# A decoder block on one core: sums copied out of PSUM first, block transfers on the GpSimd queue, the feed-forward in emission order

## The chip, the cores and the metric

The kernel runs on one core of a Trainium2 chip. The metric is device time in microseconds; before the change it was 1412.69 us, the median of three runs (1409.19 to 1413.38).

## What is computed

One layer of a decoder for 256 tokens of width 2048 in float32: an RMS norm, one wide projection, three attention branches whose results are gated, merged and projected back, and a feed-forward with a squared ReLU. The change lies in the feed-forward, the last line here:

```python
h = _rms(x, g_mix_norm[layer])
z = h @ w_in[layer]
...                                   # three attentions from z: oa, ob, oc
merged = (gates[:, :, 0] * (oa @ w_up_a[layer])
          + gates[:, :, 1] * (ob @ w_up_b[layer])
          + gates[:, :, 2] * (oc @ w_up_c[layer]))
x = x + merged @ w_out[layer]
h2 = _rms(x, g_ffn_norm[layer])       # 256 x 2048; w_ff_in is 2048 x 8192, w_ff_out 8192 x 2048
x = x + jnp.square(jax.nn.relu(h2 @ w_ff_in[layer])) @ w_ff_out[layer]
```

## The kernel before

**Matmuls and splits.** Every weight is split into two parts, `whi` (ScalarE casts it to float32r) and `wlo` (VectorE subtracts that from the weight), and so is every activation. A product is three passes: high by high, low by high, high by low. `wload` loads a plain weight tile (two 128-row slices of 512 columns) through SP's DMA queue into `raw` and splits it. The pools `raw`, `whi` and `wlo` have four buffers each. `wahead` keeps the splits of up to two further tiles written ahead of the matmuls of the current one, by the order of `plan`.

**Feed-forward.** The 8192 hidden columns are worked off in four quarters, q = 0 to 3. q = 0 has four plain strips of w_ff_in (`strip_rows`), two plain strips of w_ff_out and one unit of w_ff_out. Each later q has two units of w_ff_in and two of w_ff_out, so there are 13 units.

**A unit** (`unit`) computes 256 rows by 1024 columns. For six of its sixteen 128-row slices it uses a Winograd form of the 2 x 2 block product: seven block products instead of eight (B11, T2, T3, T1, B21, B22, T4), each in two parts of two slices and one slice (`SUBS`). The other ten slices come as ten plain tiles. `UNIT` is the order: B11, three plain, T2, plain, T3, plain, T1, plain, B21, plain, B22, plain, T4, two plain; with the parts counted singly 24 places, numbered 0 to 23. `uload` makes the block sums T3, T2, T1 and T4 of the weights on VectorE (1536 elements each) and splits them; the blocks lie in six `sraw` buffers that `fetch` fills, through SP's queue too. B11, T2, T3 and T1 go to PSUM banks of their own (`pp`): the first two in the pool `ps_sc`, T3 and T1 in `ps_tp`, which has two buffers and also serves the transposes. After T1 `early` combines these (`partial_sums`: `p1s`, `uu` twice, `wz`); in w_ff_out three additions into the residual `x1` follow. At the last two plain places `late` ends the four accumulators: in w_ff_in VectorE adds (`y`), and ScalarE takes ReLU and square; in w_ff_out VectorE adds into `x1`.

**Hidden tiles.** `hidden_rows` is a generator that `pump` moves on by one step after each place: transposes of a `y` on TensorE into a `tp` of `ps_tp`, then the split into `hid`. The tiles 0 and 1 of each q also give the activation sums of the next w_ff_out unit: `sums_of` reads both `tp` of such a tile straight from PSUM, with a copy `a21s` on ScalarE and four operations on VectorE, and splits the result into `ss`. `split_rows` does the same once for the input of w_ff_in (`sx`).

**What sets the order.** Nothing is ordered by hand: the scheduler of the framework puts each engine's instructions in an order that it works out with a timing model, and it may move an instruction ahead of others that were written earlier. The line numbers below are those of the profile; the helper `split_into` gives its lines 275 and 276 to whatever is split through it.

Of the kernel before, what the change touches and what calls it, by code (L numbers as in the profile page):

```python
# [11 lines left out]
F32 = mybir.dt.float32  # L12
F32R = mybir.dt.float32r
AF = mybir.ActivationFunctionType
ALU = mybir.AluOpType
# [3 lines left out]
P = 128  # L19
# [26 lines left out]
SH = 3  # L46
K1, K2 = [0, 1, 4], [2, 3, 5]
SUBS = [(0, 2), (2, 1)]
# [46 lines left out]
def tile_block(ctx: ExitStack, tc: tile.TileContext, io):  # L95
    nc = tc.nc
# [29 lines left out]
    posts, attn = deque(), deque()  # L126

    def step(queue):
        try:
            next(queue[0][1])  # L130
        except StopIteration:
            queue.popleft()
# [6 lines left out]
    def drain(queue, label):  # L139
        while any(l == label for l, _ in queue):  # L140
            step(queue)
# [26 lines left out]
    last_load = [None]  # L168
# [24 lines left out]
    def fetch(u, n):  # L193

        if u == len(units):
            return
        name, at = units[u]
        size = P * SH * 512
        got = ready.setdefault(u, {})
        for i, k in enumerate(list(BLOCKS)[len(got):n], len(got)):  # L200
            off = (at * len(BLOCKS) + i) * size
            got[k] = pool[0].tile([P, SH, 512], F32, tag="sraw", name="sraw")
            last_load[0] = nc.sync.dma_start(
                got[k], io[name][off:off + size].rearrange("(p g n) -> p g n", p=P, g=SH)).ins

    def uload(name, which):

# [64 lines left out]
    def split_into(hi, lo, src, scale=None):  # L272

        if scale is None:
            nc.scalar.copy(hi, src)  # L275
            nc.vector.tensor_tensor(lo, src, hi.bitcast(F32), op=ALU.subtract)  # L276
        else:
            nc.scalar.activation(hi, src, AF.Copy, scale=scale)  # L278
            nc.vector.scalar_tensor_tensor(lo, src, scale, hi.bitcast(F32), op0=ALU.mult, op1=ALU.subtract)

    def unit(name, sums, xh, xl, early, late):


# [359 lines left out]
    for t in range(2):  # L643
        nc.vector.scalar_tensor_tensor(zf[:, t, :], acc[t][:, 256:260], rstd[:, t:t + 1], bf,
                                       op0=ALU.mult, op1=ALU.add)
# [71 lines left out]
    ff = ctx.enter_context(tc.tile_pool(name="ff", bufs=1))  # L717
# [4 lines left out]
    for c in range(4):  # L722
# [6 lines left out]
        for j in range(2):  # L729
            tp = ps_tp.tile([P, 2, S], F32, tag="tp", name="tp")  # L730
# [18 lines left out]

    x1h, x1l = rows_of(x1T)  # L750

    S_USE = {"T1": 0, "T2": 1, "T3": 2, "B22": 3}

    def sums_of(a, ss):

        (a11, a12), (a21, a22) = a
        n = ss.shape[3]
        sf = ff.tile([P, 4, n, P], F32, tag="sf", name="sf", bufs=1)
        a21s = ff.tile([P, n, P], F32, tag="a21", name="a21s", bufs=1)
        nc.scalar.copy(a21s, a21)  # L760
        nc.vector.tensor_tensor(sf[:, 0], a22, a21s, op=ALU.add)  # L761
        nc.vector.tensor_tensor(sf[:, 2], a11, a21s, op=ALU.subtract)
        nc.vector.scalar_tensor_tensor(sf[:, 1], a11, -1.0, sf[:, 0], op0=ALU.mult, op1=ALU.add)
        nc.vector.tensor_tensor(sf[:, 3], a12, sf[:, 1], op=ALU.subtract)
        split_into(ss[:, 0], ss[:, 1], sf)

    def sums_for(at, ss):

        sums = {k: (lambda hl, g, i=i: ss[:, hl, i, g, :]) for k, i in S_USE.items()}
        sums["B11"] = lambda hl, g: at(K1[g], hl, slice(0, P))  # L770
# [4 lines left out]
    def partial_sums(p1, p6, p7, p5):  # L775
        p1s = ff.tile([P, 512], F32, tag="p1", name="p1s", bufs=1)
        uu = ff.tile([P, 2, 512], F32, tag="uu", name="uu", bufs=1)
        wz = ff.tile([P, 2, 512], F32, tag="wz", name="wz", bufs=1)
        nc.scalar.copy(p1s, p1)
        nc.vector.tensor_tensor(uu[:, 0, :], p6, p1s, op=ALU.add)  # L780
        nc.vector.tensor_tensor(uu[:, 1, :], p7, uu[:, 0, :], op=ALU.add)
        nc.vector.tensor_tensor(wz, p5[:, None, :].to_broadcast([P, 2, 512]), uu, op=ALU.add)
        return p1s, uu[:, 1, :], wz

    def hidden_rows(ys, hh, ss, wait):

        for _ in range(wait):
            yield
        tps = []
        for t in range(2):  # L790
            yield
            tp = ps_tp.tile([P, 4, P], F32, tag="tp", name="tp")
            for i in range(4):
                nc.tensor.transpose(tp[:, i, :], ys[t][:, i * P:(i + 1) * P], ident)  # L794
            ts = slice(t * P, (t + 1) * P)
            split_into(hh[:, :, 0, ts], hh[:, :, 1, ts], tp)
            tps.append(tp)
        if ss is not None:
            yield
            g0, n = SUBS[ss[1]]  # L800
            sums_of([[tp[:, n * i:n * i + n, :] for i in range(2)] for tp in tps], ss[0][:, :, :, g0:g0 + n, :])


    rrow = ff.tile([P, S], F32, name="rrow")
    sx = ff.tile([P, 2, 4, SH, P], F32R, name="sx")
# [16 lines left out]
            scaled.append(f)  # L822

    def split_rows():
        yield
        for g, f in enumerate(scaled):
            yield
            split_into(x1T[:, 4 * g:4 * g + 4, 0, :], x1T[:, 4 * g:4 * g + 4, 1, :], f)
            if g < len(SUBS):
                yield  # L830
                g0, n = SUBS[g]
                sums_of([[f[:, n * j:n * j + n, i * P:(i + 1) * P] for j in range(2)] for i in range(2)],
                        sx[:, :, :, g0:g0 + n, :])

    for q in range(4):
        hid = [ff.tile([P, 4, 2, S], F32R, tag="hid", name="hid", bufs=4) for _ in range(4)]
        ss = ff.tile([P, 2, 4, SH, P], F32R, tag="ss", name="ss", bufs=1)
        for sidx in range(4 if q == 0 else 0):
            if sidx == 1:
                attn.append(("x", scale_rows()))  # L840
            acc = strip_rows("w_ff_in", 512, KT, x1h, x1l)
            ys = []
            for t in range(2):
                y = ff.tile([P, 512], F32, tag="y", name="y", bufs=4)
                nc.scalar.activation(y, acc[t], AF.Relu, scale=ss2[:, t:t + 1])
                nc.scalar.activation(y, y, AF.Square)
                ys.append(y)
            posts.append(("h", hidden_rows(ys, hid[sidx], (ss, sidx) if sidx < len(SUBS) else None, 1)))
        for u in range(2 if q else 0):
            more = {}  # L850

            def early(*p):
                more[0, 0], more[0, 1], wz = partial_sums(*p)
                more[1, 0], more[1, 1] = wz[:, 0, :], wz[:, 1, :]

            def late(c, t, acc):
                y = ff.tile([P, 512], F32, tag="y", name="y", bufs=4)
                nc.vector.tensor_tensor(y, acc, more[c, t], op=ALU.add)
                nc.scalar.activation(y, y, AF.Relu)
                nc.scalar.activation(y, y, AF.Square)  # L860
                more["y", t] = y
                if t:
                    i = 2 * u + c
                    posts.append(("h", hidden_rows([more["y", 0], y], hid[i], (ss, i) if i < len(SUBS) else None,
                                                   0 if c else 2)))

            unit("w_ff_in", sums_for(lambda kt, hl, ts: x1T[:, kt, hl, ts], sx), x1h, x1l, early, late)
        if q == 0:
            drain(attn, "x")
            attn.append(("x", split_rows()))  # L870
        hidh = lambda kt, t: hid[kt // 4][:, kt % 4, 0, t * P:(t + 1) * P]
        hidl = lambda kt, t: hid[kt // 4][:, kt % 4, 1, t * P:(t + 1) * P]
        for c in range(0 if q else 2):
            acc = strip_rows("w_ff_out", 512, KT, hidh, hidl)
            cs = slice(c * 512, (c + 1) * 512)
            for t in range(2):
                nc.vector.tensor_tensor(x1[:, t, cs], acc[t], x1[:, t, cs], op=ALU.add)
        for u in range(0 if q else 1, 2):
            cols = [slice(1024 * u + 512 * c, 1024 * u + 512 * (c + 1)) for c in range(2)]

            def early(*p):
                p1s, u3, wz = partial_sums(*p)
                nc.vector.tensor_tensor(x1[:, 0, cols[0]], p1s, x1[:, 0, cols[0]], op=ALU.add)
                nc.vector.tensor_tensor(x1[:, 1, cols[0]], u3, x1[:, 1, cols[0]], op=ALU.add)
                nc.vector.tensor_tensor(x1[:, :, cols[1]], wz, x1[:, :, cols[1]], op=ALU.add)

            def late(c, t, acc):
                nc.vector.tensor_tensor(x1[:, t, cols[c]], acc, x1[:, t, cols[c]], op=ALU.add)  # L888
                if q == 3:
                    load(io["out"][t * P:(t + 1) * P, cols[c]], x1[:, t, cols[c]])  # L890

            unit("w_ff_out", sums_for(lambda kt, hl, ts: hid[kt // 4][:, kt % 4, hl, ts], ss), hidh, hidl, early, late)
        drain(attn, "x")
# [71 lines left out]
```

## Time and profile before

| | us |
|---|---|
| median of three runs | 1412.69 |
| profiled execution | 1411.21 |
| span of that execution | 1409.4 |
| TensorE busy | 1393.0 (99%) |
| VectorE busy | 1024.9 (73%) |
| ScalarE busy | 759.9 (54%) |
| GpSimd busy | 37.5 (3%) |

The first unit starts at about 842 us. From there on VectorE is busy for nine tenths of the time, TensorE nearly throughout. In the profile PE is TensorE, DVE VectorE, ACT ScalarE and SP the engine whose queue carries nearly all loads. A matmul's end is modelled and overlaps the next one's start, so that the distance between starts is its cost, not its duration. "Idle before" names the engine whose work ended the wait.

### The profile page before, as it was taken

To read this page: it belongs to the slowest core of one execution; us is meant where nothing else is said; L and a number is where in the kernel's file an instruction comes from. 1 tells how busy PE (TensorE), PEld (TensorE's weight loads), DVE (VectorE), ACT (ScalarE), POOL (GpSimd) and SP (SyncE) were. 2 spreads that over 40 slices of the span, in tenths; PEclk is the share of its full clock that TensorE was granted. 3 is DMA by queue.
4 is the path that set the end of the run, shared out by engine and by line. 5 is a ranking of instruction groups with operands and counts; after the bars stand their busy time and mean duration, and the time that the engine had idled before them with its cause. 6 is when DMAs were issued, how large, how long until landed. Compare 5 with 4: busy or idle time off the path is not lost.

```text
span 1409.4 us, 17262 instructions
## 1 busy us (share of the span) xinstructions
PE 1393.0 (99%) x6343; PEld 1153.1 (82%) x6343; DVE 1024.9 (73%) x1167; ACT 759.9 (54%) x983; POOL 37.5 (3%) x41
## 2 busy tenths in 40 slices
PE   8999999999999999999999999999999999999998
PEld 6888888888888888888888888878888788887887
DVE  6647657566755646565567758899988899988996
ACT  7545545466444444444455635566555665556653
POOL 0211102000000000000000000000000000000000
PEclk9999999999999999999999999999999999999999
DMA  9747555655566666676675755655666556665562
GB/s 326 239 139 239 169 148 165 197 184 165 182 207 198 199 200 200 196 233 204 183 231 180 228 188 185 219 186 176 200 210 198 172 184 206 207 191 181 187 207 77
DMA packets 75524, 274.54 MB, mean 195 GB/s; under 512 B 8624, under 2 KB 9392, under 8 KB 75184
## 3 DMA queue, kind: packets, MB, share of 16 engines
q1 hardware_dynamic: 75296, 273.42, 60.6%
q8 instruction: 50, 0.82, 0.2%
q14 instruction: 34, 0.28, 0.1%
q10 hardware_dynamic: 144, 0.02, 0.0%
HBM read 271.31 MB, written 2.10 MB: 194 GB/s over the span
## 4 chain that ended last, share of the span: by engine, by line
PE 73%; DVE 0%; ACT 0%; issue 0%
PE acc L265 33%; PE acc L292 31%; PE pp L292 8%; PE tp L794 1%; PE tp L734 0%; PE tp L706 0%; DVE hid L276 0%; ACT hid L275 0%; DVE sf L761 0%; ACT a21s L760 0%; DVE x L888 0%; PE rr L813 0%
## 5 line engine op out<-in xcount | busy, mean ns | idle before, releaser
L188 DVE TENSOR_TENSOR wlo<-raw,whi 128x1024 fp32r<-128x1024 f32 (+2 forms) x425 | 509.6, 1204 | 283.1 <-ACT whi L187 274.2
L187 ACT CAST whi<-raw 128x1024 fp32r<-128x1024 f32 (+2 forms) x425 | 441.3, 1039 | 455.9 <-PE acc L265 313.7
L265 PE MATMUL acc<-whi,xT 128*128 128x512 f32 (+1 forms) x1472 | 393.6, 389 | 5.7 <-ACT xT L278 5.4
L265 PEld LDWEIGHTS acc<-whi,xT 128*128 128x128 f32 x1472 | 272.7, 189 | 61.5 <-ACT xT L278 6.1
L265 PE MATMUL acc<-wlo,xT 128*128 128x512 f32 (+1 forms) x736 | 226.2, 388 | 0.0
L275 ACT CAST whi<-sraw 128x1024 fp32r<-128x1024 f32 (+1 forms) x182 | 151.0, 837 | 115.3 <-PE acc L292 83.4
L276 DVE TENSOR_TENSOR wlo<-sraw,whi 128x1024 fp32r<-128x1024 f32 (+1 forms) x182 | 169.8, 953 | 22.2 <-ACT whi L275 16.4
L292 PE MATMUL acc<-whi,hid 128*128 128x512 f32 x644 | 166.4, 391 | 0.0
L265 PEld LDWEIGHTS acc<-wlo,xT 128*128 128x128 f32 x736 | 136.9, 188 | 28.1 <-issue 1.0
L292 PE MATMUL acc<-whi,x1T 128*128 128x512 f32 x552 | 140.7, 391 | 0.0
L292 PEld LDWEIGHTS acc<-whi,hid 128*128 128x128 f32 x644 | 120.3, 188 | 24.5
L292 PEld LDWEIGHTS acc<-whi,x1T 128*128 128x128 f32 x552 | 103.2, 188 | 21.2
L292 PE MATMUL acc<-wlo,hid 128*128 128x512 f32 x322 | 91.1, 390 | 0.0
L292 PE MATMUL acc<-wlo,x1T 128*128 128x512 f32 x276 | 76.9, 390 | 0.0
L292 PEld LDWEIGHTS acc<-wlo,hid 128*128 128x128 f32 x322 | 60.2, 188 | 12.4
L265 PE MATMUL acc<-whi,x1T 128*128 128x512 f32 x256 | 70.0, 394 | 0.0
L265 PE MATMUL acc<-whi,mT 128*128 128x512 f32 x256 | 69.9, 392 | 0.0
L265 PE MATMUL acc<-whi,oT 128*128 128x512 f32 x224 | 60.0, 390 | 0.6 <-ACT oT L278 0.6
L292 PEld LDWEIGHTS acc<-wlo,x1T 128*128 128x128 f32 x276 | 51.6, 188 | 10.6
L265 PEld LDWEIGHTS acc<-whi,mT 128*128 128x128 f32 x256 | 47.9, 188 | 9.6
L265 PEld LDWEIGHTS acc<-whi,x1T 128*128 128x128 f32 x256 | 47.5, 188 | 9.4
L265 PEld LDWEIGHTS acc<-whi,oT 128*128 128x128 f32 x224 | 42.0, 188 | 9.6 <-ACT oT L278 0.9
(201 smaller groups left out, 1337.5 us busy)
## 6 DMA issues: line engine op xcount, KB each, us to landing
raw<-in_w_gate_dram SPq DMA_DIRECT2D x96, 512.0 KB, 3.6
raw<-in_w_ff_in_dram SPq DMA_DIRECT2D x92, 512.0 KB, 4.1
raw<-in_w_ff_out_dram SPq DMA_DIRECT2D x86, 512.0 KB, 4.3
raw<-in_w_proj_dram SPq DMA_DIRECT2D x77, 512.0 KB, 3.9
sraw<-in_w_ff_out_blocks_dram SPq DMA_DIRECT2D x28, 768.0 KB, 4.5
sraw<-in_w_ff_in_blocks_dram SPq DMA_DIRECT2D x24, 768.0 KB, 5.5
raw<-in_w_out_dram SPq DMA_DIRECT2D x32, 512.0 KB, 3.5
raw<-in_w_up_c_dram SPq DMA_DIRECT2D x12, 512.0 KB, 3.5
```

The lines of the kernel that those rows point to most:

```text
L187: nc.scalar.copy(hi[:, gs, :], raw[:, gs, :])
L188: nc.vector.tensor_tensor(lo[:, gs, :], raw[:, gs, :], hi[:, gs, :].bitcast(F32), op=ALU.subtract)
L265: nc.tensor.matmul(acc[t][:, :n], lhsT=xs(kt, t), rhs=ws[:, g, :], start=(first and kt == 0), stop=(last and kt == nkt - 1),)
L275: nc.scalar.copy(hi, src)
L276: nc.vector.tensor_tensor(lo, src, hi.bitcast(F32), op=ALU.subtract)
L292: nc.tensor.matmul(acc, lhsT=x(hl, g), rhs=w[:, g, :], start=(first and i == 0 and g == 0), stop=(last and i == 2 and g == n - 1))
L794: nc.tensor.transpose(tp[:, i, :], ys[t][:, i * P:(i + 1) * P], ident)
```

## The change

Three things. `keep` copies the transposed tiles out of PSUM into one float32 tile `sf` (ScalarE, right behind the split), and `sums_of` works on `sf`, in four VectorE operations and one split for all three slices of a quarter, as a generator of its own that `pump` moves on; the places of T3, T2 and T1 in it are renamed to fit. The blocks' transfers are issued from GpSimd's queue. And from the feed-forward's loop on, the instructions of TensorE, VectorE and ScalarE stand in the order in which the code emits them, without the scheduler.

```diff
@@ fetch
-            last_load[0] = nc.sync.dma_start(
-                got[k], io[name][off:off + size].rearrange("(p g n) -> p g n", p=P, g=SH)).ins
+            nc.gpsimd.dma_start(got[k], io[name][off:off + size].rearrange("(p g n) -> p g n", p=P, g=SH))
@@ sums_of
-        a21s = ff.tile([P, n, P], F32, tag="a21", name="a21s", bufs=1)
-        nc.scalar.copy(a21s, a21)
-        nc.vector.tensor_tensor(sf[:, 0], a22, a21s, op=ALU.add)
-        nc.vector.tensor_tensor(sf[:, 2], a11, a21s, op=ALU.subtract)
-        nc.vector.scalar_tensor_tensor(sf[:, 1], a11, -1.0, sf[:, 0], op0=ALU.mult, op1=ALU.add)
-        nc.vector.tensor_tensor(sf[:, 3], a12, sf[:, 1], op=ALU.subtract)
-        split_into(ss[:, 0], ss[:, 1], sf)
+        yield
+        op(2, 0, 2, ALU.add)
+        op(0, 1, 0, ALU.subtract)
+        yield
+        op(1, 2, 1, ALU.subtract)
+        op(3, 3, 1, ALU.subtract)
+        yield
+        nc.scalar.copy(ss[:, 0], sf)
+        yield
+        nc.vector.tensor_tensor(ss[:, 1], sf, ss[:, 0].bitcast(F32), op=ALU.subtract)
+
+    def keep(sf, i, t, src):
+        g0, n = SUBS[i]
+        nc.scalar.copy(sf[:, 1 - t::2, g0:g0 + n, :], src.rearrange("p (h g) n -> p h g n", h=2))
@@ hidden_rows
             split_into(hh[:, :, 0, ts], hh[:, :, 1, ts], tp)
-            tps.append(tp)
-        if ss is not None:
-            yield
-            g0, n = SUBS[ss[1]]
-            sums_of([[tp[:, n * i:n * i + n, :] for i in range(2)] for tp in tps], ss[0][:, :, :, g0:g0 + n, :])
+            if sf is not None:
+                keep(sf[0], sf[1], t, tp[:, :2 * SUBS[sf[1]][1], :])
+                if t and sf[1] == len(SUBS) - 1:
+                    attn.append(("s", sums_of(sf[0], sf[2])))
@@ the loop over q
+    ET = mybir.EngineType
+    ctx.enter_context(tc.manual_schedule(engines={ET.PE, ET.DVE, ET.Activation}))
     for q in range(4):
...
+        drain(attn, "s")
```

The order of the built programs differs from the first unit on. The lines of the changed kernel differ by a few from those of the kernel before: 274 and 275 there are 275 and 276 here.

ScalarE at the end of the first w_ff_in unit of q = 1, before (`y` is ReLU and square, `whi` a weight split, raw a plain tile and sraw a block):

```order
L187 CAST whi<-raw 128x1024 x2
L859 ACTIVATE y<-y 128x512 x2
L860 ACTIVATE y<-y 128x512
L187 CAST whi<-raw 128x1024
L860 ACTIVATE y<-y 128x512
L859 ACTIVATE y<-y 128x512
L275 CAST whi<-sraw 128x1024
L779 COPY p1s<-pp 128x512
L859 ACTIVATE y<-y 128x512
L275 CAST whi<-sraw 128x512
L860 ACTIVATE y<-y 128x512 x2
```

The same place in the changed kernel:

```order
L187 CAST whi<-raw 128x1024 x2
L274 CAST whi<-sraw 128x1024
L867 ACTIVATE y<-y 128x512
L868 ACTIVATE y<-y 128x512
L867 ACTIVATE y<-y 128x512
L868 ACTIVATE y<-y 128x512
L274 CAST whi<-sraw 128x512
L867 ACTIVATE y<-y 128x512
L868 ACTIVATE y<-y 128x512
L867 ACTIVATE y<-y 128x512
L868 ACTIVATE y<-y 128x512
L187 CAST whi<-raw 128x1024 x2
```

The eight operations on `y` stood between three weight splits; now four stand ahead of the split of place 1 of the next unit, and four more ahead of that of place 2.

VectorE around `early` of the w_ff_out unit of q = 0, before (L780, L781 and L782 are `uu`, `uu` and `wz`, L884 and L885 additions into `x1`):

```order
L780 TENSOR_TENSOR uu<-pp,p1s 128x512
L188 TENSOR_TENSOR wlo<-raw,whi 128x1024
L276 TENSOR_TENSOR wlo<-sraw,whi 128x1024
L276 TENSOR_TENSOR wlo<-sraw,whi 128x512
L781 TENSOR_TENSOR uu<-pp,uu 128x512
L188 TENSOR_TENSOR wlo<-raw,whi 128x1024
L884 TENSOR_TENSOR x_5018<-uu,x_5018 128x512
L276 TENSOR_TENSOR wlo<-sraw,whi 128x1024
L276 TENSOR_TENSOR wlo<-sraw,whi 128x512
L782 TENSOR_TENSOR wz<-pp,uu 128x1024
L188 TENSOR_TENSOR wlo<-raw,whi 128x1024
L885 TENSOR_TENSOR x_5018<-wz,x_5018 128x2x512
```

The same place in the changed kernel (L229 is the block sum T4, L230 before):

```order
L275 TENSOR_TENSOR wlo<-sraw,whi 128x1024
L787 TENSOR_TENSOR uu<-pp,p1s 128x512
L788 TENSOR_TENSOR uu<-pp,uu 128x512
L789 TENSOR_TENSOR wz<-pp,uu 128x1024
L892 TENSOR_TENSOR x_5018<-p1s,x_5018 128x512
L893 TENSOR_TENSOR x_5018<-uu,x_5018 128x512
L894 TENSOR_TENSOR x_5018<-wz,x_5018 128x2x512
L275 TENSOR_TENSOR wlo<-sraw,whi 128x512
L229 TENSOR_TENSOR sraw<-sraw 128x1536
L188 TENSOR_TENSOR wlo<-raw,whi 128x1024
```

The sums and additions, which stood between weight splits, now stand in one piece between the splits of places 14 and 15; the block sum T4 stands ahead of the split of place 16, where before it came ahead of all these rows.

TensorE in the same unit, T2's last part and the plain tile behind it, before and then changed:

```order
L292 MATMUL pp<-wlo,ss 128x512
L292 MATMUL acc<-whi,hid 128x512 x8
L292 MATMUL acc<-wlo,hid 128x512 x4
L292 MATMUL pp<-whi,ss 128x512 x4
L292 MATMUL pp<-wlo,ss 128x512 x2
```

```order
L291 MATMUL pp<-wlo,ss 128x512
L291 MATMUL acc<-whi,hid 128x512 x4
L291 MATMUL acc<-wlo,hid 128x512 x2
L291 MATMUL acc<-whi,hid 128x512 x4
L291 MATMUL acc<-wlo,hid 128x512 x2
L291 MATMUL pp<-whi,ss 128x512 x4
```

Before, a plain tile's low part was wanted after eight matmuls with the high part; now after four.

## Rows read from the trace of the kernel before

**Rows 1.** The page: each engine's busy time and share; one group (count | busy, mean ns).

```profile
PE 1393.0 (99%) x6343; PEld 1153.1 (82%) x6343; DVE 1024.9 (73%) x1167; ACT 759.9 (54%) x983; POOL 37.5 (3%) x41
...
L292 PE MATMUL acc<-whi,hid 128*128 128x512 f32 x644 | 166.4, 391 | 0.0
```

**Rows 2.** Waits of TensorE, feed-forward: who waited for whom, us, times, longest.

```profile
PE pp L292 <- DVE sf L761: 6.3, 3, 2.1
```

**Rows 3.** The chain around the three waits: start, us, what.

```profile
946.65 0.45 PE tp L794 x4
...
947.12 0.59 ACT hid L275
...
947.74 0.70 DVE hid L276
...
948.76 0.30 DVE sf L761
...
949.20 4.37 PE pp L292 x18
...
1118.74 0.45 PE tp L794 x4
...
1121.29 5.93 PE pp L292 x18
...
1292.47 0.45 PE tp L794 x4
...
1295.02 5.97 PE pp L292 x18
```

**Rows 4.** The chain's last long piece of matmuls.

```profile
1385.92 19.73 PE acc L292 x87
```

**Rows 5.** Stretches: length, busy PE, PEld, DVE, ACT, POOL; clock, DMA share, GB/s.

```profile
970.00:1012.00 42.00, 42.00 (x195) 34.80 (x194) 38.60 (x41) 27.29 (x37) 0.00 (x0) 1.00 0.58 188
...
1100.00:1200.00 100.00, 97.89 (x441) 80.69 (x440) 90.57 (x100) 63.95 (x84) 0.00 (x0) 0.98 0.56 184
```

**Rows 6.** VectorE by shape, 842 to 1405.8 us: count | busy, mean ns | idle before.

```profile
L276 DVE TENSOR_TENSOR wlo<-sraw,whi 128x512 fp32r<-128x512 f32 x90 | 61.7, 686 | 2.7 <-ACT whi L275 2.0
L230 DVE TENSOR_TENSOR sraw<-sraw 128x1536 f32<-128x1536 f32 x13 | 22.8, 1756 | 0.4
...
L782 DVE TENSOR_TENSOR wz<-pp,uu 128x1024 f32<-128x1024 f32 x13 | 15.8, 1219 | 2.1 <-PE pp L292 2.1
...
L780 DVE TENSOR_TENSOR uu<-pp,p1s 128x512 f32<-128x512 f32 x13 | 8.9, 684 | 0.0
...
L883 DVE TENSOR_TENSOR x<-p1s,x 128x512 f32<-128x512 f32 x7 | 4.8, 682 | 0.0
...
L761 DVE TENSOR_TENSOR sf<-tp,a21s 128x256 f32<-128x256 f32 x3 | 1.2, 416 | 0.0
```

**Rows 7.** ScalarE by shape, the same stretch and columns.

```profile
L275 ACT CAST whi<-sraw 128x512 fp32r<-128x512 f32 x90 | 55.9, 621 | 52.5 <-PE acc L292 30.1 <-PE pp L292 19.2 <-DVE x L885 3.0
...
L779 ACT COPY p1s<-pp 128x512 f32<-128x512 f32 x13 | 7.5, 574 | 0.0
```

**Rows 8.** VectorE in order of time: start, us, what.

```profile
927.98 0.68 DVE L858 TENSOR_TENSOR y<-acc,uu 128x512 f32<-128x512 f32 x1
928.58 1.21 DVE L188 TENSOR_TENSOR wlo<-raw,whi 128x1024 fp32r<-128x1024 f32 x1
929.71 1.28 DVE L858 TENSOR_TENSOR y<-acc,wz 128x512 f32<-128x512 f32 x2
```

**Rows 9.** ScalarE in order of time; and its plain splits by shape.

```profile
928.10 1.23 ACT L859 ACTIVATE y<-y 128x512 f32<-128x512 f32 x2 [0.41 <-DVE y L858]
...
L187 ACT CAST whi<-raw 128x1024 fp32r<-128x1024 f32 x130 | 137.0, 1054 | 98.5 <-PE acc L292 69.2 <-PE pp L292 20.1 <-PE acc L265 3.8
```

**Rows 10.** Blocks: transfer's time to landing; VectorE's waits for them.

```profile
DMA to landing us min/median/max: 4.1/4.7/6.6
...
DVE sraw L216 <- DMA sraw<-in_w_ff_in_blocks_dram: 10.3, 6, 2.8
```

More of the change, by code (lines that the diff above doesn't have):

```diff
@@ L750, in tile_block, with sums_of, op @@
     x1h, x1l = rows_of(x1T)
[L752 to L758, printed above, removed]
-        a21s = ff.tile([P, n, P], F32, tag="a21", name="a21s", bufs=1)
-        nc.scalar.copy(a21s, a21)
-        nc.vector.tensor_tensor(sf[:, 0], a22, a21s, op=ALU.add)
-        nc.vector.tensor_tensor(sf[:, 2], a11, a21s, op=ALU.subtract)
-        nc.vector.scalar_tensor_tensor(sf[:, 1], a11, -1.0, sf[:, 0], op0=ALU.mult, op1=ALU.add)
-        nc.vector.tensor_tensor(sf[:, 3], a12, sf[:, 1], op=ALU.subtract)
-        split_into(ss[:, 0], ss[:, 1], sf)
+    S_USE = {"T3": 0, "T2": 1, "T1": 2, "B22": 3}
+    def sums_of(sf, ss):
+        def op(dst, a, b, how):
+            nc.vector.tensor_tensor(sf[:, dst], sf[:, a], sf[:, b], op=how)
+        yield
[11 more added lines that the diff above has]
+        nc.scalar.copy(sf[:, 1 - t::2, g0:g0 + n, :], src.rearrange("p (h g) n -> p h g n", h=2))
     def sums_for(at, ss):
@@ L783, in partial_sums, with hidden_rows @@
         return p1s, uu[:, 1, :], wz
-    def hidden_rows(ys, hh, ss, wait):
+    def hidden_rows(ys, hh, sf, wait):
         for _ in range(wait):
             yield
-        tps = []
         for t in range(2):
@@ L824, in split_rows @@
     def split_rows():
+        sfx = ff.tile([P, 4, SH, P], F32, tag="sf", name="sf", bufs=1)
         yield
@@ L829, in split_rows @@
             if g < len(SUBS):
[L830 to L833, printed above, removed]
+                for t in range(2):
+                    keep(sfx, g, t, f[:, :2 * SUBS[g][1], t * P:(t + 1) * P])
+        yield from sums_of(sfx, sx)
+    ET = mybir.EngineType
+    ctx.enter_context(tc.manual_schedule(engines={ET.PE, ET.DVE, ET.Activation}))
     for q in range(4):
@@ L837, in tile_block @@
         ss = ff.tile([P, 2, 4, SH, P], F32R, tag="ss", name="ss", bufs=1)
+        sf = ff.tile([P, 4, SH, P], F32, tag="sf", name="sf", bufs=1)
         for sidx in range(4 if q == 0 else 0):
@@ L847, in tile_block @@
                 ys.append(y)
-            posts.append(("h", hidden_rows(ys, hid[sidx], (ss, sidx) if sidx < len(SUBS) else None, 1)))
+            posts.append(("h", hidden_rows(ys, hid[sidx], (sf, sidx, ss) if sidx < len(SUBS) else None, 1)))
         for u in range(2 if q else 0):
@@ L863, in late @@
                     i = 2 * u + c
-                    posts.append(("h", hidden_rows([more["y", 0], y], hid[i], (ss, i) if i < len(SUBS) else None,
+                    posts.append(("h", hidden_rows([more["y", 0], y], hid[i], (sf, i, ss) if i < len(SUBS) else None,
                                                    0 if c else 2)))
```

## The prediction

> **What bounds the kernel now.** Read the page's first part, then the waits of TensorE, then the chain. TensorE is busy 99% of the span [rows 1], and the only thing in the feed-forward that it waits for is a subtraction of `sums_of`: three times, 6.3 us in all [rows 2]. The chain shows where: after the last four transposes of a hidden tile the product T3 wants the PSUM buffer that the transposes filled, and that one is held until ScalarE and VectorE have split it and `sums_of` has read it [rows 3]. Back to back, a 512-column matmul takes 19.73 / 87 = 0.227 us and four transposes 0.45 [rows 3, 4], so the 18 matmuls of T3 and T1 should end 0.45 + 4.08 = 4.53 us after the transposes begin. They end 6.92, 8.48 and 8.52 us after: 2.39 + 3.95 + 3.99 = **10.3 us** lost. The second and third lose more than the wait because the granted clock was at the lower of its two levels for a while behind it (5.93 and 5.97 us for the 18 matmuls, not 4.08; a mean clock of 0.98 from 1100 to 1200 us, which hold the second) [rows 3, 5]. Elsewhere TensorE has no hole, so 10.3 us is all that can be won.
>
> VectorE is the next engine: 38.6 us busy in the 42 us of one feed-forward unit [rows 5]. That it costs TensorE nothing rests on its order.
>
> **Removing the wait: minus 10.3 us.** The copies out of PSUM (`keep`) go to ScalarE, four in a second unit of a q, 512 or 256 elements, at 0.57 and some 0.37 us (nearest rows: the copy p1s, and 0.42 us of VectorE for 256 elements) [rows 6, 7]. T3's buffer is then free when split and copy of the fifth tile's transposes are done, some 3 us before T3 in the working below. I take the whole 10.3; the other end, that TensorE still stands there, is 0. That the four sums now read SBUF makes them no cheaper: a 512-element VectorE operation takes 0.68 us from PSUM (uu, y) and 0.68 from SBUF (x<-p1s) [rows 6, 8]. The Trainium skill (VectorE: DVE Perf Modes, Rules for kernel authors) advises a copy from PSUM to SBUF first where many operations follow; the rows show no gain by it here, and if it halved the sums I would have 1 us of VectorE time less per q.
>
> **The emission order: what I cost.** Numbers are places in a unit: 0, 1 = B11; 2 to 4 plain; 5, 6 = T2; 7 plain; 8, 9 = T3; 10 plain; 11, 12 = T1; 13 plain; 14, 15 = B21; 16 plain; 17, 18 = B22; 19 plain; 20, 21 = T4; 22, 23 plain. A plain place is 12 matmuls, 2.72 us; a product's two places 6 and 3, 1.36 and 0.68. `wahead` writes the split of place k+3 behind everything that follows place k's matmuls, so in strict order whatever waits for place k (the ends of accumulators, pumped steps) stands ahead of the splits of k+3. The scheduler of before moved splits ahead of it and T2, T3, T1, T4 far ahead (the order rows). A VectorE operation costs its duration less 0.08, since the next starts that much earlier (1.13 for 1.21, 0.60 for 0.68) [rows 8]: 1.13 for a plain or first split, 0.60 for a second split, 1.67 for a block sum, 0.60 and 1.13 for the `uu` and `wz` sums [rows 6]. On ScalarE: split 1.05 or 0.62, relu and square 0.60 behind each other (two in 1.23) [rows 7, 9].
>
> *End of a w_ff_in unit* (6 times). Time 0 is the end of place 22 on TensorE; its result is there 0.2 later (a matmul takes 0.39 us, the next starts after 0.23) [rows 1, 4]. VectorE adds y of the second row tile to 0.88; ScalarE, busy with the first until 0.9, does relu and square to 2.1, and only then the first half of split 1 of the next unit to 2.7, VectorE the other half to 3.4. Behind that VectorE stands with the last two y, to 4.0 and 4.65; ScalarE does relu, square, relu, square from 4.1 to 6.5, and only then split 2, to 7.5. TensorE wants it after place 23, places 0 and 1 and four transposes: 2.72 + 2.04 + 0.45 = 5.2. **2.35 us x 6 = 14.1.**
>
> *T1's results in a w_ff_out unit* (`early`). Time 0: end of place 10; its buffer lets split 14 begin. ScalarE ends it at 1.25, VectorE at 2.4; behind it uu, uu, wz to 4.8, three additions into x to 7.1, split 15 to 7.7, the block sum T4 to 9.4, split 16 to 10.6. TensorE needs split 15 at 2.04 + 2.72 + 1.36 + 0.45 = 6.57 and stands 1.3; it then needs split 16 after four more matmuls, at 9.0, and stands 1.7. **3.0 us x 4 = 12.0** (the unit of q = 0 and the second of each later q). In the first w_ff_in unit of a q the three additions are missing, and only 0.6 is left: **x 3 = 1.8.**
>
> *Units behind a w_ff_in unit.* Here hidden tiles come on top and VectorE falls behind for good. From split 2 to split 16: 7 plain and 4 first splits 12.4, 4 second 2.4, 4 hidden 2.4, 4 block sums 6.7, uu and wz 2.3, and in the second w_ff_in unit the sums of the hidden tile 3.6 (4 x 0.47, between the rows for 256 and 512 elements, and 1.67); 29.8. It also stands 1.1 us twice while ScalarE splits T2 and T1, which it had to sum first, and 0.3 in small holes: 32.3. TensorE needs split 16 after 25.8 + 0.9 = 26.7 us (places 2 to 15 and three groups of transposes; four matmuls). **5.6 us x 3 = 16.8.** In the first w_ff_out unit of a q the sums are missing and the additions into x (2.3) are there: 31.0, **4.3 x 3 = 12.9.**
>
> *Once:* the two matmuls of `scale_rows` now stand side by side, and the second waits for a VectorE operation that waits for the first: 0.5.
>
> Sum 14.1 + 12.0 + 1.8 + 16.8 + 12.9 + 0.5 = 58.1; less 10.3, **plus 47.8 us**. The profiled execution took 1411.2 (span 1409.4, 1.8 around it), so 1459.0; the median stands 1.5 above it, 1412.7: **1460**. Unknown is the clock: two of three waits of 2.1 us brought the lower level, 1.9 us each. Behind a w_ff_in unit it costs nothing (VectorE is late there anyway); at the 13 halts at place 16 it costs 0 to 13 x 1.9 = 25. I take 0, since those are shorter than 2.1.
>
> **Block transfers on the GpSimd queue: 0.** 52 of them leave SP's queue, where plain loads stood between them; VectorE waited for them 10.3 us in 6 waits [rows 10], which TensorE did not feel. Nothing else is on GpSimd's queue then. They took 4.1 to 6.6 us to land [rows 10]. The tightest are B11, from the split of place 9 to the next unit's first split, and B22, from T4's sum (behind place 15) to the next T3's: 17 and 19 us of matmuls. No row shows a GpSimd transfer; below nothing it cannot help, since TensorE waits for none.
>
> **Rivals.**
> 1. *ScalarE and VectorE run ahead* of what I reckon, and the order costs nothing: 1412.7 - 10.3 = **1402**, faster. For it: ScalarE waits for TensorE's buffers most of the time [rows 9], so splits are made as soon as a buffer frees. Against: with 4 buffers nothing can be split earlier than that. It decides at 2.35 us at a w_ff_in unit's end. 0.11.
> 2. *Only the direct waits bite*, and VectorE's backlog behind w_ff_in is worked off: 14.1 + 7 x 3.0 - 10.3 = 25, **1437**. 0.13.
> 3. *Block transfers are late.* From 17 us to landing each us more is paid in 12 units: at 20 us 36 more, **1496**. The rows against it are those 4.1 to 6.6 us. 0.05. The Trainium skill (SBUF — State Buffer, two separate sides) warns that a transfer issued from GpSimd waits for its descriptors while VectorE holds the port they share (a 0.62 us one took 3.1); the same page (Who interferes with whom) exempts `tensor_tensor`, which is nearly all VectorE does here. No row of before can show it; 2.5 us more on 6.6 would still be within 17.
> 4. *They cancel*: a sixth of my sum and the 10.3 won. 0.05.
>
> **Numbers.** My forecast 0.66, with its own range 1440 to 1490 (a third of the sum too much; the clock's 25 on top). Faster by over 0.3%, which a measurement can just tell, 0.11; within 0.3% 0.05; slower 0.84. The range 1422 to 1495 leaves out rivals 1 and 4 and the tip of 3.
>
> **What would show it.** Right: TensorE no longer waits for a sum; in its place waits for ScalarE's split at place 2 behind w_ff_in units (about 2.3 us, six) and for VectorE's at places 15 and 16, more in units behind w_ff_in; VectorE's busy time nearly as before over a longer span. Wrong: those splits done before TensorE asks; or waits for `sraw`.

## The result and the profile after

The changed kernel takes **1490.11 us** (median of four runs, 1489.5 to 1490.52), the kernel before 1411.15 beside it (four runs): a ratio of 1.0559, with a 95% interval of 1.0539 to 1.0578. It is 79 us slower. The forecast was 1460, slower by 48. The time lies inside the stated range, 1422 to 1495, and just above the forecast's own, 1440 to 1490: three fifths of the loss were forecast, not all of it.

The profiled execution spans 1488.7 us, 79.3 more than before. Its page and TensorE's waits (line waited for: us in total, times, longest), which answer to [rows 1, 2]:

```profile
PE 1424.0 (96%) x6343; PEld 1156.1 (78%) x6343; DVE 1028.7 (69%) x1142; ACT 760.3 (51%) x988; POOL 64.9 (4%) x93
...
PE acc L291 <- DVE wlo L188: 15.4, 16, 1.4
PE acc L291 <- ACT whi L187: 15.2, 9, 2.2
PE acc L291 <- DVE wlo L275: 12.6, 10, 2.4
...
PE pp L291 <- DVE wlo L275: 4.6, 6, 1.1
PE pp L291 <- ACT whi L274: 4.5, 5, 1.2
```

The wait for `sf` of [rows 2] is gone. In its place stand 46 waits for split weights, `whi` from ScalarE and `wlo` from VectorE, 52.3 us together; none is for `sraw`. TensorE has as many instructions as before and VectorE's busy time rose by only 3.8 us: nothing became dearer, things became late.

The feed-forward as a whole, from 842 us on, by windows of the changed kernel and of experiment e9 below, in which TensorE has the same instructions in the same order but waits for no split (length; busy PE, PEld, DVE, ACT, POOL; granted clock, DMA share, GB/s):

```profile
842.00:1487.00 645.00, 589.57 (x2500) 464.61 (x2498) 513.04 (x516) 332.76 (x411) 25.29 (x47) 0.98 0.47 164
```

```profile
842.00:1400.00 558.00, 554.84 (x2493) 458.86 (x2491) 498.70 (x513) 336.55 (x410) 25.39 (x47) 1.00 0.58 189
```

Of the 87 us between them TensorE stands idle for 52.3 more and is "busy" for 34.7 more with the same matmuls. The second part is not work. It is the drawn-out ends of the matmuls ahead of each halt, short waits that they cover, the lower clock, and a pause behind each wait, told of below.

**The end of a w_ff_in unit.** TensorE and ScalarE in order of time, at the first of the six (start, us, what, and in brackets the idle time before and who ended it):

```profile
936.03 0.60 PE L800 MATMUL tp<-ident,y 128*128 128x128 f32 x4
938.82 1.19 PE L291 MATMUL acc<-whi,x1T 128*128 128x512 f32 x4 [2.19 <-ACT whi L187]
940.08 0.78 PE L291 MATMUL acc<-wlo,x1T 128*128 128x512 f32 x2
940.66 1.91 PE L291 MATMUL acc<-whi,x1T 128*128 128x512 f32 x4
942.37 1.06 PE L291 MATMUL acc<-wlo,x1T 128*128 128x512 f32 x2
943.22 1.00 PE L800 MATMUL tp<-ident,y 128*128 128x128 f32 x4
943.93 1.22 PE L291 MATMUL acc<-whi,x1T 128*128 128x512 f32 x4
```

```profile
935.36 0.63 ACT L867 ACTIVATE y<-y 128x512 f32<-128x512 f32 x1 [1.36 <-DVE y L866]
936.02 0.63 ACT L868 ACTIVATE y<-y 128x512 f32<-128x512 f32 x1
936.56 0.61 ACT L867 ACTIVATE y<-y 128x512 f32<-128x512 f32 x1
937.21 0.63 ACT L868 ACTIVATE y<-y 128x512 f32<-128x512 f32 x1
937.74 1.98 ACT L187 CAST whi<-raw 128x1024 fp32r<-128x1024 f32 x2
```

Four transposes take 0.45 us [rows 3], so TensorE was ready at 936.48 and went on at 938.82: 2.34 us. ScalarE, meanwhile, does the last four of eight operations on `y`, and the split that TensorE wants stands behind them in the queue.

**`early`.** VectorE and TensorE in the second w_ff_out unit of q = 1 (the unit of q = 0 has the same two halts, at 873 us):

```profile
1068.89 0.68 DVE L892 TENSOR_TENSOR x<-p1s,x 128x512 f32<-128x512 f32 x1
1069.49 0.69 DVE L893 TENSOR_TENSOR x<-uu,x 128x512 f32<-128x512 f32 x1
1070.09 1.22 DVE L894 TENSOR_TENSOR x<-wz,x 128x1024 f32<-128x1024 f32 x1
1071.23 0.69 DVE L275 TENSOR_TENSOR wlo<-sraw,whi 128x512 fp32r<-128x512 f32 x1
1071.83 1.75 DVE L229 TENSOR_TENSOR sraw<-sraw 128x1536 f32<-128x1536 f32 x1
1073.50 1.22 DVE L188 TENSOR_TENSOR wlo<-raw,whi 128x1024 fp32r<-128x1024 f32 x1
```

```profile
1071.97 0.50 PE L291 MATMUL acc<-wlo,hid 128*128 128x512 f32 x1 [1.02 <-DVE wlo L275]
1072.30 1.09 PE L291 MATMUL acc<-whi,hid 128*128 128x512 f32 x4
1074.77 0.50 PE L291 MATMUL acc<-wlo,hid 128*128 128x512 f32 x1 [1.38 <-DVE wlo L188]
```

VectorE has the split of place 15 ready only after three additions into `x`, and that of place 16 only after the block sum. TensorE stands twice. From start to start of its matmuls, less 0.227 for each, that is 1.18 and 1.54 us.

**What the forecast did not see: the copy behind a subtraction.** ScalarE and VectorE in the second w_ff_in unit of a q (`sf<-tp` at L772 is `keep`, the new copy out of PSUM; `hid` L275 is VectorE's half of the split, from the same PSUM tile):

```profile
1136.72 0.57 ACT L274 CAST hid<-tp 128x512 fp32r<-128x512 f32 x1
1138.89 0.59 ACT L772 COPY sf<-tp 128x512 f32<-128x512 f32 x1 [1.60 <-DVE hid L275]
1139.37 1.05 ACT L187 CAST whi<-raw 128x1024 fp32r<-128x1024 f32 x1
```

```profile
1138.17 0.69 DVE L275 TENSOR_TENSOR hid<-tp,hid 128x512 fp32r<-128x512 f32 x1
1140.45 1.23 DVE L188 TENSOR_TENSOR wlo<-raw,whi 128x1024 fp32r<-128x1024 f32 x1 [1.60 <-ACT whi L187]
```

Both engines only read the tile, and still ScalarE's copy starts when VectorE's subtraction has ended (1138.17 + 0.69 = 1138.86). The copy waits for a semaphore that VectorE counts up, so this order lies in the built program; whether both could read at once no run shows. VectorE reaches that subtraction late, since two splits stand ahead of it; then ScalarE's next weight split is late, and VectorE waits 1.60 us for that one in turn. A row of ScalarE's waits sums it up, 842 to 1487 us:

```profile
ACT sf L772 <- DVE hid L275: 17.1, 12, 1.6
```

The trace of the kernel before had shown the same thing in small, where `sums_of` copied a PSUM tile behind VectorE's subtraction (842 to 1409 us); the forecast made no use of it:

```profile
ACT a21s L760 <- DVE hid L276: 2.3, 3, 0.8
```

**The clock.** Windows of the changed kernel: behind the first halt, and behind the longest wait above (2.4 us), in the first w_ff_out unit of q = 1:

```profile
938.80:940.60 1.80, 1.71 (x6) 1.14 (x7) 1.80 (x2) 1.40 (x2) 0.00 (x0) 1.00 0.00 0
940.60:944.00 3.40, 3.40 (x12) 2.67 (x11) 1.80 (x3) 1.53 (x2) 0.00 (x0) 0.50 0.75 230
1026.00:1032.80 6.80, 6.01 (x15) 4.23 (x14) 5.58 (x6) 1.47 (x2) 0.54 (x1) 0.50 0.58 201
```

There are three such stretches of 3.4 us and three of 6.8, at 0.50, the lower of the two levels, 30.7 us together. In the first, six wide matmuls and four transposes (940.66 to 943.93 in TensorE's rows above) took 3.27 us, where 6 x 0.227 + 0.45 = 1.81 would do: 1.5 us lost. Worked out in the same way all six cost about 12 us beyond the halts inside them. The trace of before had lost some 3 so [rows 3, 5].

**The block transfers.** They are on another queue now, and VectorE no longer waits for them. The landing of all 52, which answers to [rows 10]:

```profile
DMA to landing us min/median/max: 4.3/4.4/8.2
```

### The profile page after: what moved, and what is told of

Read it like the earlier page. It is cut to its first block, busy times and chain, and to the rows that moved or that the text cites. A ratio compares the mean times of both kernels' runs of the same rounds, so it can differ in the third digit from the quotient of the medians.

```text
span 1488.7 us, 17184 instructions
## 1 busy us (share of the span) xinstructions
PE 1424.0 (96%) x6343; PEld 1156.1 (78%) x6343; DVE 1028.7 (69%) x1142; ACT 760.3 (51%) x988; POOL 64.9 (4%) x93
## 5 line engine op out<-in xcount | busy, mean ns | idle before, releaser
L275 DVE TENSOR_TENSOR wlo<-sraw,whi 128x1024 fp32r<-128x1024 f32 (+1 forms) x182 | 169.1, 955 | 55.2 <-ACT whi L274 53.5
L291 PE MATMUL acc<-whi,hid 128*128 128x512 f32 x644 | 181.1, 403 | 6.6 <-ACT whi L187 6.6
L291 PE MATMUL acc<-whi,x1T 128*128 128x512 f32 x552 | 151.0, 394 | 8.6 <-ACT whi L187 8.6
L291 PEld LDWEIGHTS acc<-whi,hid 128*128 128x128 f32 x644 | 124.3, 194 | 33.5 <-ACT whi L187 7.3
L291 PE MATMUL acc<-wlo,hid 128*128 128x512 f32 x322 | 105.7, 407 | 19.2 <-DVE wlo L275 11.3
L291 PE MATMUL acc<-wlo,x1T 128*128 128x512 f32 x276 | 88.6, 399 | 9.2 <-DVE wlo L188 7.5
L264 PE MATMUL acc<-whi,x1T 128*128 128x512 f32 x256 | 69.8, 393 | 0.0
```

What stands on the lines that cost most here:

```text
L264: nc.tensor.matmul(acc[t][:, :n], lhsT=xs(kt, t), rhs=ws[:, g, :], start=(first and kt == 0), stop=(last and kt == nkt - 1),)
L291: nc.tensor.matmul(acc, lhsT=x(hl, g), rhs=w[:, g, :], start=(first and i == 0 and g == 0), stop=(last and i == 2 and g == n - 1))
```

## The experiments

All ran three rounds beside the kernel before, whose median was 1410.6 to 1412.9 us in these groups. Where two parts of the change stand against each other, the ratio to the kernel before is given.

### The parts of the change, one by one

**e1: without the emission order.** The change is three edits: the copies, the queue, the order. This takes the third away.

```diff
-    ET = mybir.EngineType
-    ctx.enter_context(tc.manual_schedule(engines={ET.PE, ET.DVE, ET.Activation}))
```

> The changed kernel with the scheduler's order back (sums copied out of PSUM and GpSimd queue stay). Theory (the emission order costs everything, the copies only take the three waits for the sums away): 1401 us, that is 10 below the kernel before, and no wait of TensorE for a sum. Rival (the copies on ScalarE or the GpSimd queue cost time themselves): above 1411.

Measured: 1401.51 us, ratio 0.9929 (0.9913 to 0.9946), and no wait of TensorE in the feed-forward. The copies and the queue gain what the waits of [rows 2, 3] had cost, 10.3 us; the order turns that into a loss.

**e2: the emission order alone**, put into the kernel before.

```diff
+    ET = mybir.EngineType
+    ctx.enter_context(tc.manual_schedule(engines={ET.PE, ET.DVE, ET.Activation}))
     for q in range(4):
```

> The kernel before with nothing but the emission order for TensorE, VectorE and ScalarE. Theory: it halts as the changed kernel does at the ends of the w_ff_in units (6 x 2.35) and at T1's results (some 2.7 in four units), so 1465 to 1495. Rival (the order hurts only because ScalarE's copies stand in it): within 5 of 1411.

Measured: 1493.54 us, ratio 1.0582 (1.055 to 1.0613), the same within the intervals as the whole change. The halts of 2.35 us at the ends of the w_ff_in units are there as well.

**e3: the block transfers back on SP's queue.**

```diff
-            nc.gpsimd.dma_start(got[k], io[name][off:off + size].rearrange("(p g n) -> p g n", p=P, g=SH))
+            last_load[0] = nc.sync.dma_start(
+                got[k], io[name][off:off + size].rearrange("(p g n) -> p g n", p=P, g=SH)).ins
```

> The changed kernel with the blocks' transfers back on SP's queue. Theory (the GpSimd queue is off every path): 1490, within 4. Rival (block transfers from GpSimd come late or slow VectorE): 10 or more below 1490. Third possibility: blocks queued behind plain loads now hold VectorE in its fixed order, 5 or more above 1490.

Measured: 1491.88 us, ratio 1.0569 (1.0546 to 1.0591). The queue is worth nothing that these intervals can tell, either way.

**e8: the copies alone** (the edits of e1 and e3 together).

> The kernel before with the sums copied out of PSUM and nothing else: scheduler's order, blocks on SP's queue. Theory (the copies alone take the three waits away): 1401 to 1403, as e1_scheduler. Rival (the GpSimd queue brought the gain in e1_scheduler): 1409 to 1413.

Measured: 1402.28 us, ratio 0.993 (0.9913 to 0.9948). The gain of e1 is that of the copies, with the sums rewritten to work on them; the two weren't taken apart.

### Which queues hold the lateness

**e9: emission order on TensorE alone; e10: on VectorE and ScalarE alone.** The forecast put the loss down to VectorE's and ScalarE's queues. It could as well have been TensorE's own, in which the products are no longer moved to where their operands are ready.

```diff
-    ctx.enter_context(tc.manual_schedule(engines={ET.PE, ET.DVE, ET.Activation}))
+    ctx.enter_context(tc.manual_schedule(engines={ET.PE}))
```

```diff
-    ctx.enter_context(tc.manual_schedule(engines={ET.PE, ET.DVE, ET.Activation}))
+    ctx.enter_context(tc.manual_schedule(engines={ET.DVE, ET.Activation}))
```

> The changed kernel with TensorE alone in emission order; VectorE and ScalarE are left to the scheduler. My theory is that the halts come from the queues of VectorE and ScalarE, where splits of weights stand behind activations, additions and sums that are written ahead of them; with those two free the splits are early again although TensorE's matmuls stand exactly as in the changed kernel: 1400 to 1412 us, and next to no waits of TensorE for whi or wlo in the feed-forward. The rival is that TensorE's own order costs (the products T2, T3, T1 and T4 and the transposes no longer moved to where they are ready): then the halts stay and it is 1460 to 1490 us.

> The changed kernel with VectorE and ScalarE in emission order and TensorE left to the scheduler. My theory: the splits are as late as in the changed kernel, and moving matmuls can't make a split earlier by more than the matmuls that don't need it: 1450 to 1490 us, with TensorE waiting for whi and wlo. If TensorE's own order is what costs: 1400 to 1415 us. If only both together cost, both runs are near 1402.

Measured: e9 1402.69 us, ratio 0.9943 (0.9928 to 0.9958); e10 1477.35 us, ratio 1.0474 (1.0456 to 1.0491). This is the cleanest pair of the study: in e9 TensorE's instructions stand in the changed kernel's order, one by one, and it stands for none of its splits. TensorE is busy for 99% of its span, as before the change. ScalarE at the end of the first w_ff_in unit:

```profile
929.48 0.62 ACT L867 ACTIVATE y<-y 128x512 f32<-128x512 f32 x1
930.01 1.04 ACT L187 CAST whi<-raw 128x1024 fp32r<-128x1024 f32 x1
930.95 0.63 ACT L868 ACTIVATE y<-y 128x512 f32<-128x512 f32 x1
```

The split that came behind eight operations on `y` in the changed kernel now runs among them, at 930.01, and is there when TensorE has done its transposes. In e10, TensorE's waits from 842 us on:

```profile
PE acc L291 <- ACT whi L187: 24.4, 9, 3.5
PE acc L291 <- DVE wlo L188: 6.0, 12, 0.6
PE pp L291 <- ACT whi L274: 5.4, 6, 1.6
PE acc L291 <- DVE wlo L275: 1.7, 3, 0.6
```

With TensorE free to take other matmuls first, waits for `wlo` shrink from 32.6 to 7.7 us, but the wait for ScalarE's split of `raw` grows, and only 12 of the 79 us come back (1.0559 - 1.0474 of 1411). So the fixed order of VectorE and ScalarE costs nearly all of it; that of TensorE costs nothing by itself, and beside the other takes away 12 us of room to go on with other matmuls. Whether VectorE's order or ScalarE's alone would cost as much was not tried.

### The sizes of single terms

**e4: `keep` ahead of VectorE's subtraction.** The rival to "the copy waits behind VectorE" is that VectorE has simply more to do than was reckoned.

```diff
-            split_into(hh[:, :, 0, ts], hh[:, :, 1, ts], tp)
+            nc.scalar.copy(hh[:, :, 0, ts], tp)
             if sf is not None:
                 keep(sf[0], sf[1], t, tp[:, :2 * SUBS[sf[1]][1], :])
+            nc.vector.tensor_tensor(hh[:, :, 1, ts], tp, hh[:, :, 0, ts].bitcast(F32), op=ALU.subtract)
+            if sf is not None:
```

> The changed kernel with ScalarE's copy out of PSUM ahead of VectorE's subtraction from the same PSUM tile. Theory (in the second w_ff_in unit of a q ScalarE stands waiting for VectorE's subtraction with weight splits behind it; that is why the halts there are 9 us and not the 5.6 reckoned): about 3 us less in each of three such units, 1478 to 1483. Rival (VectorE's plain amount of work sets these halts): within 3 of 1490.

Measured: 1482.41 us, ratio 1.0502 (1.048 to 1.0525). ScalarE now goes from one to the next:

```profile
1137.11 0.58 ACT L802 CAST hid<-tp 128x512 fp32r<-128x512 f32 x1
1137.58 0.59 ACT L772 COPY sf<-tp 128x512 f32<-128x512 f32 x1
1138.06 1.06 ACT L187 CAST whi<-raw 128x1024 fp32r<-128x1024 f32 x1
```

The halts in the three second w_ff_in units fall from 26.4 to 19.1 us, where the forecast had 16.8. So three quarters of what that term lacked is this wait, and 2.3 us of it are not; the time fell by 8 us, as expected. By the ratios the changed kernel is 3 us faster than e2, the order without the copies, and e4 is 11 faster (each uncertain by some 5), which fits a wait that takes back most of the 10.7 us that the copies gain in e8. The two readers of the tile still go one after the other: VectorE's subtraction at 1141.27 now waits 0.89 us for ScalarE's copy, but the copy is short and nothing that TensorE needs soon stands behind it.

**e5: splits first** at two places: a further `wahead(3)` ahead of the last sums of a unit (`late`) and ahead of `early`, so that a split ahead stands in front of activations and additions.

```diff
+                    wahead(3)
```

> The changed kernel, still in emission order, but one more weight split written ahead of the ends of accumulators (late) and of T1's results (early). Theory (what stands ahead of the splits makes the halts): no halt at the six ends of w_ff_in units (14.1 us), at most half of the 2.7 at T1's results in four units, and fewer falls of the clock behind them; 1450 to 1470. Rival (VectorE's amount of work makes the halts, whatever the order): within 8 of 1490, the halts only moved.

Measured: 1474.03 us, ratio 1.0435 (1.042 to 1.0451): 16 us of gain, less than the theory's range and more than the rival's. `early` behaved: 2.72 us fell to one halt of 1.2, and the 0.51 of the first w_ff_in unit of a q went. But at the ends of units the halts only moved (two rows of TensorE):

```profile
941.78 1.20 PE L291 MATMUL acc<-whi,x1T 128*128 128x512 f32 x4 [1.95 <-ACT whi L187]
...
1003.15 1.20 PE L291 MATMUL pp<-whi,ss 128*128 128x512 f32 x4 [2.59 <-ACT whi L274]
```

The first stands two plain places further on and is 2.1 us from start to start instead of 2.35; the second, at T2 of the next unit, is new. ScalarE's eight operations on `y` must run somewhere, and in a fixed order whatever is behind them waits.

**e6: e4 and e5 together.**

> The edit of e5_splits_first and that of e4_keep_first together. Theory (two separate queues behind two separate waits): both gains add, so 6 to 10 below e5_splits_first. Rival (both free the same ScalarE time): as e5_splits_first.

Measured: 1467.6 us, ratio 1.039 (1.0369 to 1.041), 6.4 below e5: most of e4's gain comes on top, so the two waits are separate.

**e7: TensorE kept busy at unit ends.** At each of the six, the four transposes are repeated five more times (20 transposes, some 2.3 us), into the same tile and with the same values, where TensorE stands anyway. If the lower clock comes from its standing, the stretches behind those halts should go.

```diff
-            for i in range(4):
+            for i in list(range(4)) * (6 if wait == 2 and t == 0 else 1):
```

> The changed kernel with the transposes at the head of each of the six w_ff_in unit ends done six times over (20 more, 2.2 us, into the same tile), so that TensorE works through the 2.35 us in which it stood. Theory (the stretches at the lower clock behind these ends come from TensorE standing): the three stretches of 3.4 us behind the unit ends are gone, the longer ones behind T1's results in the first w_ff_out units stay, 1484 to 1488. Rival (they come from something else): the stretches stay, within 2 of 1490. If the wait were not the weight split's, the added transposes would come on top: 1500.

Measured: 1489.18 us (1488.69 to 1492.99), ratio 1.0549 (1.0529 to 1.0569), no difference that these intervals can tell from the changed kernel's. Windows of it:

```profile
939.20:944.00 4.80, 4.74 (x24) 3.88 (x23) 3.20 (x5) 2.24 (x4) 0.00 (x0) 1.00 0.66 213
1270.40:1273.80 3.40, 2.98 (x7) 2.40 (x8) 3.24 (x4) 0.02 (x1) 0.31 (x1) 0.50 0.72 211
```

The mechanism held: all three 3.4-us stretches behind unit ends are gone (the first row is the place of the second row of the clock's windows above). But one new stretch appeared elsewhere, so that 30.7 us at the lower level became 23.9; at 1.5 us for a stretch of 3.4, two of them fewer are worth 3 us. By the ratios 1.4 came (1.0559 - 1.0549 of 1411), uncertain by about 4, so the price is neither confirmed nor denied, and the expected time was missed. The new stretch lies around a halt of 1.37 us:

```profile
1270.82 1.22 PE L291 MATMUL acc<-wlo,hid 128*128 128x512 f32 x2 [1.37 <-DVE wlo L188]
```

The same halt in the changed kernel, at 1272.73 and of 1.38 us, brought none. So a halt of TensorE can bring the lower level, and which one does is not settled by its length alone.

## Why the prediction was right in sign and short in size

Halts here are measured from start to start of TensorE's matmuls, less 0.227 us for each.

| step of the prediction | forecast, us | measured, us |
|---|---|---|
| the waits for `sums_of`, removed | -10.3 | -11.3 (e1), -10.7 (e8), -8.0 (e9) |
| ends of w_ff_in units | 6 x 2.35 = 14.1 | 6 x 2.35 = 14.1 |
| `early`, w_ff_out units | 4 x 3.0 = 12.0 | 4 x 2.72 = 10.9 |
| first w_ff_in unit of a q | 3 x 0.6 = 1.8 | 3 x 0.51 = 1.5 |
| second w_ff_in units, backlog | 3 x 5.6 = 16.8 | 8.0 + 9.2 + 9.2 = 26.4 |
| first w_ff_out units, backlog | 3 x 4.3 = 12.9 | about 12.9 |
| `scale_rows` | 0.5 | 1.8 |
| block transfers on GpSimd's queue | 0 | 0 (e3, e8) |
| lower clock | 0 (bound 25) | about 12, 9 more than before |
| pauses of 0.11 us behind waits | not thought of | about 6.7 more than before |

Together: 47.8 forecast, + 9.6 (second w_ff_in units), - 1.4 (`early` and the first w_ff_in units), + 1.3 (`scale_rows`), + 12 (clock; before's own 3 are in the 10.3 removed), + 6.7 (pauses) make 76.0 of the 79.3 by which the span grew. Some 3 us stay unassigned.

**What was right.** The mechanism, shown by e9 and e10: with VectorE and ScalarE in emission order, a split stands behind everything written ahead of it. Working through the two queues operation by operation, with durations from the trace of before, gave the end of a unit step by step: counted from the end of place 22 (931.27 in the first such unit), ScalarE's last four operations on `y` start at 4.09 us and the split behind them at 6.47, where the prediction has 4.1 and 6.5. That the halt agrees to a hundredth is luck, since its steps are rounded to tenths. In `early` the first of the two halts is by the prediction's own times 7.7 - 6.57 = 1.1, not 1.3, and measures 1.18. The missing three additions set the 2.72 and the 0.51 apart as forecast. The signs that it named came: waits for ScalarE's split at place 2 (2.35 us, six) and for VectorE's at places 15 and 16, none for `sraw`.

Rival 1, 1402 us, is what the change gives with VectorE and ScalarE left to the scheduler. Against rival 2, the backlog behind w_ff_in units is real. Rival 3 did not come: the transfers landed in 4.3 to 8.2 us, far from 17, and e3 shows the queue to be free. The Trainium skill (SBUF — State Buffer, Who interferes with whom) exempts `tensor_tensor` from holding up GpSimd's transfers; nearly all of VectorE's work here is that, and the trace agrees: a block landed after 4.4 us in the median, and after 4.2 from SP's queue in e3. That 1490 still lies inside the range is in part luck: its upper end had 25 us of room for the clock, which took about half; the wait of `keep` and the pauses, which the prediction did not have, took the rest.

**What was wrong, first: the price of `keep`.** The prediction costed the copies by their busy time, 0.57 and 0.37 us of ScalarE. The step failed because it asked only how long they take and not what they wait for: each is queued behind VectorE's subtraction from the same tile, 1.4 to 1.6 us in eleven cases of the twelve and 0.8 in one, and ScalarE's next weight split behind it. e4 takes that wait away, and the term falls from 26.4 to 19.1; the 2.3 us over the forecast's 16.8 no run takes apart. The advice of the Trainium skill (VectorE: DVE Perf Modes, Rules for kernel authors) to copy out of PSUM first where many operations follow did pay here, but not by cheaper operations: in e8 VectorE's busy time is 1022.2 us against 1024.9 [rows 1], and the 10.7 us gained are those of [rows 2, 3], where the product T3 waited for its PSUM buffer. The copy hands it back earlier.

**Second: the clock.** The prediction had 0 to 25 us and took 0, with the reason that behind a w_ff_in unit the lower level costs nothing, since VectorE is late there anyway. Three of the six halts at unit ends were followed by 3.4 us at the lower level and each first w_ff_out unit by 6.8. The value to take was between the ends: the waits of 2.1 us of [rows 3] had brought it in two cases of three, and the forecast itself had six halts of 2.35 and bigger sums. e7 supports the cause (it takes the three stretches away). How much of the 1.5 us of such a stretch is hidden, as the prediction said, the quarters q = 1 to 3 tell. Behind the first unit's end only q = 1 has a stretch: from that halt's end to the restart behind the halt at place 16, 38.15 us pass there (938.82 to 976.97) and 37.77 in q = 2 and 3. Behind the second unit's end q = 2 and 3 have one: 30.61 us from that halt's end to the end of the wait of 2.4 (1192.70 to 1223.31), against 29.37 in q = 1. So the stretch costs 0.4 us behind the first unit, where the prediction's nothing is nearly right, and 1.2 behind the second in the other two quarters. What is hidden there stands in a shorter halt at T2 behind it, 0.18 us against 1.38 and 1.36, and so in the 8.0 of the table against 9.2.

**Third: the restart.** The first group behind a halt is slower at the full clock too: at 938.82 four matmuls take 1.26 us to the next group's start and the next two 0.58, where back to back it is 0.91 and 0.45. What happens there shows in TensorE's weight loads (PEld; it loads the activations), two rows at this place, and then those waits from 842 to 1487 us that are more than in the matmuls' rows:

```profile
938.82 0.76 PEld L291 LDWEIGHTS acc<-whi,x1T 128*128 128x128 f32 x4 [2.42 <-ACT whi L187]
940.08 0.30 PEld L291 LDWEIGHTS acc<-wlo,x1T 128*128 128x128 f32 x2 [0.50 <-DVE wlo L188]
...
PEld acc L291 <- DVE wlo L188: 27.2, 25, 1.8
PEld pp L291 <- DVE wlo L275: 13.2, 18, 1.5
PEld pp L291 <- ACT whi L274: 8.0, 12, 1.5
```

Half of the 0.48 us is a second wait: VectorE's part of the late split begins only when ScalarE's has ended, at 938.80, and ends at 940.03, when TensorE has been through with the four matmuls for 0.2 us. There are 28 more waits in the loads' rows than in the matmuls' (25, 18 and 12 against 16, 6 and 5); those in the two rows of backlog are part of what was measured there. The other half is two pauses of about 0.11 us, each behind the first matmul after a wait. Back to back a load starts with the matmul ahead of its own; behind a wait it starts with its own (both at 938.82), and the next only 0.11 us later, so that one load isn't hidden. There are 82 such pauses in the changed kernel (8.8 us), 66 of them right behind a wait and 11 behind transposes, and 23 before (2.05 us); in 80 of the 82 the load starts with its own matmul. The prediction took a halt to cost one wait for one split; it costs some tenths more.

**Fourth, small:** the two matmuls of `scale_rows` wait 1.8 us for VectorE instead of the 0.5 reckoned.

## What to carry to other kernels

A fixed order of emission has to be judged on the engines that feed the bottleneck, not on the bottleneck: walk their queues operation by operation, and ask for each operand that the bottleneck wants what is written ahead of it. Cost an added copy by what it must wait for on the tile that it reads, and by what is queued behind it, before its own duration. Here the part of the change worth keeping is the copy out of PSUM with the scheduler left on (e1, e8: 0.993 of the time before, faster than both kernels).

## What the runs showed of the hardware that was not expected

- A wait of TensorE costs more than its length: one pause of about 0.11 us behind the first matmul after it, at a granted clock of 1.00, since the weight load that is hidden back to back starts with its own matmul there (66 of the 82 pauses in the changed kernel stand right behind a wait, 11 behind transposes).
- The lower clock level came for 3.4 or 6.8 us at a time in the rows seen here. It followed halts of 2.35 us three times out of six, and came around one of 1.37 us in e7 where the same place in the changed kernel had none; e7, which filled the halts at unit ends with repeated transposes, had none at those places. A stretch of 3.4 us lost 1.5 us in its rows but only 0.4 to 1.2 by the end of the next unit's halts; in the first case a later halt was shorter by 1.2.
- A block of 768 KB lands equally soon from GpSimd's queue (median 4.4 us, at most 8.2) and from SP's (4.2, at most 7.9 in e3), while VectorE is busy 80% of the feed-forward (513.04 of 645 us).
